# Two ties in the feed-forwards and another first block: a float32 decoder layer on one core

## The chip, the cores and the metric

The kernel runs on one core of one Trainium2 chip. Its engines are TensorE (PE in the profile; PEld is its weight load), VectorE (DVE), ScalarE (ACT), GpSimd (POOL) and SyncE (SP), the last two here mostly issuing transfers. The metric is the device time in microseconds of one execution, as the median of several. The time before is 1223.34 us (three runs, 1223.24 to 1223.8).

## The reference

One layer on 512 tokens of width 1024, all in float32:

```python
f = swiglu(rms_norm(h, ffn1_norm_pre[l]), ffn1_w_gate[l], ffn1_w_up[l], ffn1_w_down[l])
h = h + 0.5 * rms_norm(f, ffn1_norm_post[l])
u = rms_norm(h, mix_norm_pre[l])
proj = u @ w_in[l]
...                                  # dilated attention and a gated linear recurrence
h = h + rms_norm(merged @ w_out[l], mix_norm_post[l])
f = swiglu(rms_norm(h, ffn2_norm_pre[l]), ffn2_w_gate[l], ffn2_w_up[l], ffn2_w_down[l])
h = h + 0.5 * rms_norm(f, ffn2_norm_post[l])

def swiglu(x, w_gate, w_up, w_down):
    return (jax.nn.silu(x @ w_gate) * (x @ w_up)) @ w_down
```

The feed-forwards have 2816 hidden columns, 22 chunks of 128. The change lies in the two feed-forwards and in the very first block of the first.

## The kernel before

**Products.** A float32 matmul is made of three: each operand is split into a high part, which ScalarE writes with a rounding copy (`L269`), and a low part, which VectorE gets by subtraction (`L270`). TensorE adds high x high, high x low and low x high into one bank (`mm3`, L284 to L286; the same three at L1008 to L1010 and L922 to L924).

**The beginning.** The first six gate and up products go column block by column block of x, eight blocks k of 128. `fetch_start` loads for each k a weight block ("first" for k = 0, which also carries the gains, then "raw") and the rows `h`, all issued by SP in turn. Per k, ScalarE splits the weight, scales the rows by the gain into their high part (L361, `pre_norm`) and squares them for the norm; VectorE makes both low parts (L270, L362) and sums the squares. Four banks accumulate. Ahead of it, `WARM` matmuls on a constant tile (L1144, two rows of the trace each) keep TensorE busy while the first loads are under way.

**Chunks of a feed-forward.** From chunk f = 6 of the first (f = 3 of the second) gate and up of a chunk are computed together with seven half-size products instead of eight, in `prod`: p1, p5, p6, p2, p7, p3, p4, each twelve matmuls of 128x256. They share three banks. b takes p1, p6, p7, p4; z (bank 5) takes p5, then p3; y takes p2. Between them stand reads of a bank before the next product adds to it: ScalarE copies b to y after p1 (L1029), z to c5 after p5 and b to c6 after p6 (both L1016); VectorE reads b + c5 between p7 and p4 (L1021) and z + c6 after p3 (L1021). Thus p3 cannot begin before the copy c5 is taken, nor p4 before L1021 on b.

**Windows.** The down projection of the chunks already made is also done in seven products, in `step`, each on 128x512 rows (L922 to L924, banks 3, 4, 6, 7). Between two chunks there is a window of two or three of these steps. In the first feed-forward the first windows follow chunks 7 to 12 (the table `LEAD`: steps p1, p2, p5, then p6, p7, then p3, p4, and once more). Their weights come in by GpSimd's transfers into the tiles npair and dr, some of them adding to what lies there (L879, L881), and are split into `wd` (`down_form`) for the coming window, tied behind the copy c6.

**What sets the order.** A scheduler puts each engine's instructions in one fixed order, by priorities (`tc.high_priority`) and by when it reckons their inputs to be there. A tie, `tc.issue_after(i)`, forces what is issued inside it behind instruction i on i's engine. `behind(...)` ties to the last product (PE), the last silu (ACT) or the last gating multiply (DVE) of the chunk before:

```python
lead = f == n0
with behind("PE"):
    product("p1", b, True)
...
with behind("DVE", "ACT"):
    forms[ev[1]] = w_forms_in_place(("gu", n, ev[1]))
```

The first says that a chunk's p1 comes after the window ahead of it. The second holds back the weight forms of the next chunk: splits on ScalarE and VectorE (L269, L270) and sums on VectorE (L654 to L658). `last`, which the ties refer to, starts empty, so a feed-forward's first forms have no tie.

**The boundary.** Ahead of the second feed-forward, `Boundary.block` makes each of four token blocks: VectorE forms h (L475), ScalarE its sum of squares (L478), VectorE the normed rows u (L483). `Boundary.turn` transposes them on TensorE (L491), four matmuls to a bank and two banks to a block, and splits them (L494, L495, a copy L496). Blocks 2 and 3 are turned while the feed-forward's first products run on blocks 0 and 1 (`gemm_first`).

## Time and profile before

| | |
|---|---|
| median of three runs | 1223.34 us |
| the profiled execution's own time | 1223.28 us |
| its span | 1221.2 us |
| TensorE busy | 1209.9 us, 99% |
| VectorE busy | 984.0 us, 81% |
| ScalarE busy | 746.0 us, 61% |
| mean granted clock | 0.999 |

The span runs from the first instruction to the last; the own time holds 2.1 us more around it. A row of the timeline gives start, duration, engine, line, operation, output and input tiles with their shapes, and, in brackets, idle time of that engine just before with what ended it. Tile names carry no buffer numbers: `w`, `wd` and `bank` stand for several tiles each. Matmuls overlap, so a matmul's duration is longer than the distance to the next one's start.

### The profile page before, as it was taken

What the parts mean: (1) busy time and instruction counts of PE and PEld (TensorE: products, weight loads), DVE (VectorE), ACT (ScalarE), POOL (GpSimd) and SP (SyncE); (2) the same over time, 40 slices, a digit from 0 to 9 for tenths busy, and PEclk for the clock granted to TensorE, in tenths of its full rate; (3) what the DMA queues carried; (4) which work ended last, traced back from release to release, by engine and by line L of the source; (5) the groups of instructions that cost most, each with busy time, mean ns of one, the idle gap of its engine ahead of it and who ended that gap; (6) DMA issues with size and microseconds to landing.
All of it is one profiled execution on the core that took longest, in us unless ns stands there. A gap on an engine that the chain in (4) does not pass through costs nothing.

```text
span 1221.2 us, 19573 instructions
## 1 busy us (share of the span) xinstructions
PE 1209.9 (99%) x7790; PEld 1102.6 (90%) x7790; DVE 984.0 (81%) x1540; ACT 746.0 (61%) x1238; POOL 84.5 (7%) x139
## 2 busy tenths in 40 slices
PE   9999999999999999999999999999999999999998
PEld 8898989999878899999999888888899999999996
DVE  7998878988579888888776998755789887979864
ACT  6566665655656564666666788634566665656452
POOL 0001111100102000000001000000110110101000
PEclk9999999999999999999999999999999999999999
DMA  6336646464735222223235223524462655555441
GB/s 247 138 104 173 170 111 171 141 163 121 255 116 176 105 82 101 78 79 104 70 138 202 75 91 141 183 101 164 132 190 87 182 155 146 159 136 163 114 156 69
DMA packets 37452, 167.63 MB, mean 137 GB/s; under 512 B 4209, under 2 KB 7665, under 8 KB 25329
## 3 DMA queue, kind: packets, MB, share of 16 engines
q1 hardware_dynamic: 18432, 107.13, 25.2%
q0 software_dynamic: 18928, 59.25, 18.1%
q8 instruction: 61, 1.00, 0.3%
q14 instruction: 31, 0.25, 0.1%
HBM read 153.79 MB, written 8.39 MB: 133 GB/s over the span
## 4 chain that ended last, share of the span: by engine, by line
PE 93%; DVE 4%; issue 1%; DMA 1%; ACT 1%; DVEq 0%; ACTq 0%
PE bank L1008 10%; PE bank L1009 9%; PE bank L1010 9%; PE bank L284 7%; PE bank L286 7%; PE bank L285 7%; PE bank L675 6%; PE bank L676 6%; PE bank L677 6%; PE bank L923 4%; PE bank L922 4%; PE bank L924 4%; PE bank L405 3%; PE bank L406 3%; PE bank L404 3%; DVE w L270 1%
## 5 line engine op out<-in xcount | busy, mean ns | idle before, releaser
L270 DVE TENSOR_TENSOR w<-raw,w 128x1024 fp32r<-128x1024 f32 (+1 forms) x276 | 300.6, 1100 | 61.9 <-ACT w L269 56.0
L269 ACT ACTIVATE w<-raw 128x1024 fp32r<-128x1024 f32 (+1 forms) x276 | 258.9, 956 | 102.4 <-PE bank L286 40.1
L1008 PE MATMUL bank<-big,w 128*128 128x256 f32 x840 | 240.6, 286 | 2.5 <-ACT c L1016 0.9
L1009 PE MATMUL bank<-big,w 128*128 128x256 f32 x840 | 237.5, 283 | 0.0
L1010 PE MATMUL bank<-big,w 128*128 128x256 f32 x840 | 236.2, 283 | 0.0
L1008 PEld LDWEIGHTS bank<-big,w 128*128 128x128 f32 x840 | 160.8, 191 | 7.3 <-ACT c L1016 1.9
L1009 PEld LDWEIGHTS bank<-big,w 128*128 128x128 f32 x840 | 160.9, 192 | 1.6
L1010 PEld LDWEIGHTS bank<-big,w 128*128 128x128 f32 x840 | 160.3, 192 | 0.0
L922 PE MATMUL bank<-wd,act 128*128 128x512 f32 x224 | 87.8, 392 | 0.0
L923 PE MATMUL bank<-wd,act 128*128 128x512 f32 x224 | 87.8, 392 | 0.0
L924 PE MATMUL bank<-wd,act 128*128 128x512 f32 x224 | 87.2, 389 | 0.0
L675 PE MATMUL bank<-big,w 128*128 128x256 f32 x252 | 73.0, 290 | 0.0
L677 PE MATMUL bank<-big,w 128*128 128x256 f32 x252 | 71.5, 284 | 0.0
L676 PE MATMUL bank<-big,w 128*128 128x256 f32 x252 | 71.2, 283 | 0.0
L1016 ACT ACTIVATE c<-bank 128x256 f32<-128x256 f32 x72 | 27.5, 382 | 61.3 <-PE bank L1010 60.8
L270 DVE TENSOR_TENSOR wd<-npair,wd 128x1024 fp32r<-128x1024 f32 x24 | 29.4, 1224 | 37.7 <-ACT wd L269 37.7
L284 PE MATMUL bank<-act,w 128*128 128x512 f32 (+1 forms) x168 | 58.6, 354 | 0.0
L285 PE MATMUL bank<-act,w 128*128 128x512 f32 (+1 forms) x168 | 58.5, 349 | 0.0
L286 PE MATMUL bank<-act,w 128*128 128x512 f32 (+1 forms) x168 | 58.5, 349 | 0.0
L284 PE MATMUL bank<-big,w 128*128 128x512 f32 x144 | 56.0, 389 | 0.0
L285 PE MATMUL bank<-big,w 128*128 128x512 f32 x144 | 56.0, 389 | 0.0
L286 PE MATMUL bank<-big,w 128*128 128x512 f32 x144 | 56.0, 389 | 0.0
(399 smaller groups left out, 3208.7 us busy)
## 6 DMA issues: line engine op xcount, KB each, us to landing
raw<-in_w SPq DMA_DIRECT2D x90, 1024.0 KB, 4.9
dr<-in_wdn POOLq DMA_DIRECT2D x40, 512.0 KB, 5.8
npair<-in_wdn POOLq DMA_DIRECT2D x32, 512.0 KB, 5.5
big<-act POOLq DMA_DIRECT2D x6, 512.0 KB, 4.1
h<-in_x SPq DMA_DIRECT2D x8, 256.0 KB, 5.2
h<-in_xn POOLq DMA_DIRECT2D x4, 512.0 KB, 5.2
raw<-in_wbig SPq DMA_DIRECT2D x2, 1024.0 KB, 4.8
kept_m<-h POOLq DMA_DIRECT2D x4, 512.0 KB, 2.9
```

What stands on the lines that cost most here:

```text
L269: ACT.activation(dh, src, AF.Copy)
L270: DVE.tensor_sub(dl, src, dh.bitcast(F32))
L284: PE.matmul(ps, wh, xh, start=first, stop=False)
L285: PE.matmul(ps, wh, xl, start=False, stop=False)
L286: PE.matmul(ps, wl, xh, start=False, stop=last)
L675: PE.matmul(ps, wh, xh, start=start and k == 0, stop=False, skip_group_check=True)
L676: PE.matmul(ps, wh, xl, start=False, stop=False, skip_group_check=True)
L677: PE.matmul(ps, wl, xh, start=False, stop=k == 3, skip_group_check=True)
L922: PE.matmul(ps, xh, wh, start=start and k == 0, stop=False, skip_group_check=True)
L1008: PE.matmul(ps, wh, xh, start=start and k == 0, stop=False, skip_group_check=True)
L1009: PE.matmul(ps, wh, xl, start=False, stop=False, skip_group_check=True)
L1010: i = PE.matmul(ps, wl, xh, start=False, stop=k == 3, skip_group_check=True)
```

## The change

1. `WARM` falls from 10 to 8.
2. The load of the first rows (k = 0) is issued by ScalarE; all others stay on SP.
3. For k = 0 VectorE makes the rows' high part with a multiply (L1154 of the changed kernel), beside ScalarE's high part of the weight. ScalarE's squares stand behind its split, VectorE's low part of the rows behind the weight's.
4. For k = 0 and 1 TensorE takes the three kinds of product one after the other over all four banks (`by_kind`), no longer bank by bank.
5. In the first feed-forward, chunks that follow a window of three steps (f = 8 and f = 11) have their p1 free; their p3 is tied behind p7 in its place.
6. The second feed-forward's `last` starts with the last VectorE and ScalarE instruction of the last `turn`, so its first weight forms stand behind these.

```diff
-WARM = 10
+WARM = 8
...
-            nc.sync.dma_start(hm(k), xT[k])
+            (nc.sync if k else nc.scalar).dma_start(hm(k), xT[k])
...
-                DVE.tensor_sub(lo, src, hi.bitcast(F32))
-                ACT.activation(fb(b, FHALVES[i]), ps, AF.Copy)
+                i_dve = DVE.tensor_sub(lo, src, hi.bitcast(F32))
+                i_act = ACT.activation(fb(b, FHALVES[i]), ps, AF.Copy)
+            self.last = {"DVE": i_dve.ins, "ACT": i_act.ins}
...
-    def ffn(n, x, r, forms_x, home, pss):
+    def ffn(n, x, r, forms_x, home, pss, after={}):
...
-        last = {}
+        last = dict(after)
...
-            with behind("PE"):
+            early = n == 1 and len(LEAD.get(f - 1, ((), ()))[1]) > 2
+            with behind(*(() if early else ("PE",))):
                 product("p1", b, True)
...
-            product("p3", z, False)
+            with behind(*(("PE",) if early else ())):
+                product("p3", z, False)
...
+    def first_rows(x, wh, wl, raw):
+        g, xh, xl = col("g1a", 0), x.hi[0], x.lo[0]
+        DVE.tensor_scalar(xh, hm(0), g, None, op0=ALU.mult)
+        i = ACT.activation(wh, raw, AF.Copy)
+        with tc.issue_after(i.ins):
+            ACT.activation(acc, hm(0), AF.Square)
+        i = DVE.tensor_sub(wl, raw, wh.bitcast(F32))
+        with tc.issue_after(i.ins):
+            DVE.scalar_tensor_tensor(xl, hm(0), g, xh.bitcast(F32), op0=ALU.mult, op1=ALU.subtract)
+        by_kind(0, wh, wl, xh, xl)
+
+    def by_kind(k, wh, wl, xh, xl):
+        for w, v in ((wh, xh), (wl, xh), (wh, xl)):
+            for j in range(4):
+                PE.matmul(pss[j], w[:, j * P:(j + 1) * P], v, start=k == 0 and w is wh and v is xh, stop=False)
...
-    end2 = ffn(2, u2, None, forms_of(u2, his, los, ap2, True), home2, pss)
+    end2 = ffn(2, u2, None, forms_of(u2, his, los, ap2, True), home2, pss, bd2.last)
```

A tie moves instructions that its own lines don't name, so three places of the fixed order follow. Lines of the changed kernel are up to 3 higher around these places (L1016 is L1017 there, L1021 is L1022, L1029 is L1031).

ScalarE in the step f=8 of the first feed-forward; `c<-bank_78` is the copy c5 of z, `bank_75<-bank_73` the copy of b to y after p1, `c<-bank_73` the copy c6, `s` the window's copies out of banks 6 and 7. Before:

```order
L1016 ACTIVATE c<-bank_78 128x256
L934 ACTIVATE s_873<-bank_79 128x512
L269 ACTIVATE act<-ub 128x512
L934 ACTIVATE s_873<-bank_80 128x512
L1029 ACTIVATE bank_75<-bank_73 128x256
L1016 ACTIVATE c<-bank_73 128x256
```

and now:

```order
L1031 ACTIVATE bank_75<-bank_73 128x256
L935 ACTIVATE s_871<-bank_79 128x512
L935 ACTIVATE s_871<-bank_80 128x512
L1017 ACTIVATE c<-bank_78 128x256
L269 ACTIVATE act<-ub 128x512
L1017 ACTIVATE c<-bank_73 128x256
```

The copy after p1 moved to the front and c5 to behind the window's copies: on TensorE p1 now fills in between the window's last matmuls, then p5, and all twelve matmuls of p3 stand between p7 and p4, where three stood.

VectorE in the step f=11; `wd_98` and `wd_99` are the two down-weight splits, `ub<-bank_74,c` the read of b + c5 ahead of p4, `g<-bank_78,c` the read of z + c6. Before:

```order
L270 TENSOR_TENSOR act<-ub,act 128x512
L1021 TENSOR_TENSOR g<-bank_78,c 128x256
L270 TENSOR_TENSOR w_1415<-raw,w_1415 128x1024
L270 TENSOR_TENSOR wd_98<-npair,wd_98 128x1024
L1021 TENSOR_TENSOR ub<-bank_74,c 128x256
L270 TENSOR_TENSOR w_1414<-raw,w_1414 128x1024
L270 TENSOR_TENSOR wd_99<-dr_100,wd_99 128x1024
```

and now:

```order
L270 TENSOR_TENSOR act<-ub,act 128x512
L270 TENSOR_TENSOR wd_98<-npair,wd_98 128x1024
L270 TENSOR_TENSOR wd_99<-dr_100,wd_99 128x1024
L1022 TENSOR_TENSOR ub<-bank_74,c 128x256
L270 TENSOR_TENSOR w_1413<-raw,w_1413 128x1024
L1022 TENSOR_TENSOR g<-bank_78,c 128x256
L270 TENSOR_TENSOR w_1412<-raw,w_1412 128x1024
```

Both down-weight splits moved in front of the read that p4 waits for; one stood there before. On TensorE p1 and p5 fill the window here as in f=8, and eleven matmuls of f=12's p5, which stood between p7 and p4, moved behind p4.

ScalarE at the last turn ahead of the second feed-forward; `w<-raw` of 512 columns is the first weight form of its first chunk. Before:

```order
L383 ACTIVATE stat<-stat 128x1
L269 ACTIVATE w_8686<-raw 128x512
L478 ACTIVATE facc,stat<-h 128x1024
L494 ACTIVATE act<-bank_80 128x4x128
L390 ACTIVATE stat<-stat,eps 128x1
L494 ACTIVATE act<-bank_78 128x4x128
```

and now:

```order
L383 ACTIVATE stat<-stat 128x1
L478 ACTIVATE facc,stat<-h 128x1024
L494 ACTIVATE act<-bank_80 128x4x128
L390 ACTIVATE stat<-stat,eps 128x1
L494 ACTIVATE act<-bank_78 128x4x128
```

The form moved behind the last `L496`; on VectorE its low part and the two sums L654 and L655, which stood ahead of the block's L495, moved behind the last L495 likewise.

More of the change, by code (lines that the diff above doesn't have):

```diff
@@ L1147, in hybrid_layer @@
     r1 = npair[:, 1, :]
+    def first_rows(x, wh, wl, raw):
[12 more added lines that the diff above has]
+                PE.matmul(pss[j], w[:, j * P:(j + 1) * P], v, start=k == 0 and w is wh and v is xh, stop=False)
     for k in range(KC):
         wh, wl, raw = wts[k]
+        if k == 0:
+            first_rows(u1, wh, wl, raw)
+            continue
         split(wh, wl, raw)
         pre_norm(u1, "g1a", k, FULL)
-        sq_add(acc, lambda s: hm(k, s), FULL, k == 0)
+        sq_add(acc, lambda s: hm(k, s), FULL, False)
         if k == KC - 1:
             rstd(acc, r1, FULL)
+        if k == 1:
+            by_kind(k, wh, wl, u1.hi[k], u1.lo[k])
+            continue
         for j in range(4):
```

## The prediction

> **What bounds the kernel now.** I read the page's busy times first, then the waits of TensorE (line waited for, total us, times, longest):

> ```profile
> PE 1209.9 (99%) x7790; PEld 1102.6 (90%) x7790; DVE 984.0 (81%) x1540; ACT 746.0 (61%) x1238; POOL 84.5 (7%) x139
> PE bank L491 <- DVE u L483: 1.4, 1, 1.4
> PE bank L1008 <- ACT c L1016: 0.9, 2, 0.5
> PE bank L1008 <- DVE u L1021: 0.9, 1, 0.9
> ```

> TensorE is the bound, and its named waits are 3.2 us in four places. All four lie where the change moves something: L491 before the second feed-forward, L1008 in the first one's steps f=8 and f=11/12. So the question is how much of these holes closes, and what opens instead. A 128x512 matmul follows its neighbour after 0.23 us (18.08 to 18.31 below), a 128x256 one after 0.12 (112.68 to 112.80). Stretches of TensorE are counted with 0.2275 and 0.12; what a stretch is longer is a hole.

> **The beginning.** Timeline rows, two matmuls from later in the same stage, the first two loads with their us to landing, one row of stretches (core row: PE, PEld, DVE, ACT, POOL, clock, DMA share, GB/s) and the nearest row for the new VectorE instruction:

> ```profile
> 0.73 1.28 ACT L356 ACT_TABLE_LOAD   x1 [0.73 <-PEq L1735]
> 1.05 4.64 PE L1144 MATMUL bank<-ones 128*128 128x128 f32 x20 [1.05 <-DVE eps L201]
> 3.75 0.63 ACT L269 ACTIVATE w<-first 128x512 fp32r<-128x512 f32 x1 [1.43 <-DMA first<-in_first]
> 4.34 0.72 ACT L361 ACTIVATE act<-h,first 128x512 fp32r<-128x512 f32 x1
> 5.34 0.77 PE L284 MATMUL bank<-act,w 128*128 128x512 f32 x1
> ...
> 18.08 0.39 PE L284 MATMUL bank<-act,w 128*128 128x512 f32 x1
> 18.31 0.39 PE L285 MATMUL bank<-act,w 128*128 128x512 f32 x1
> first<-in_first SPq DMA_DIRECT2D x1, 292.0 KB, 3.0
> h<-in_x SPq DMA_DIRECT2D x1, 256.0 KB, 3.1
> 3.00:4.00 1.00, 1.00 (x7) 1.00 (x7) 0.00 (x0) 0.25 (x1) 0.00 (x0) 1.00 0.99 376
> L1383 DVE TENSOR_SCALAR facc<-facc,w 128x256 f32<-128x256 f32 x12 | 3.5, 349 | 0.0
> ```

> The weights ("first", issued 0.74) land at 3.74, the rows (issued 1.18) at 4.28. ScalarE splits one, then the other, and is done at 5.06; the first real matmul starts at 5.34, as the warm-up ends. Now ScalarE issues the rows at 0.73, in front of its table load; an issue row of SP lasts 0.38 to 0.43, so table load and warm-up activation end near 2.8 and hide in the 1.43 us that ScalarE waits for "first". The two high parts are then made side by side: weights on ScalarE (0.63), rows on VectorE (twice 0.349, 0.70 at most).

> Two bounds. If the second queue costs "first" nothing, the operands are there at 4.4 to 4.5 and the shorter warm-up (16 rows of 0.217, to 4.5) lets TensorE start at 4.6, 0.75 early. If both share the engines, both land at 4.28 and the start is about 5.1, 0.2 early. The DMA share of 0.99 in the fourth microsecond says that there is no idle engine to use: I take 0.2. A start that early runs at half pace (0.77 for a matmul that later takes 0.39), so it is worth half: **0.1 us**, 0.4 at the early bound. Below nothing: rows that land later than now, at the price of their delay, perhaps 0.2. The new order by kinds in the first two blocks moves no total, since TensorE finds its operands there already.

> [...]

> **Step f=8.** Rows of the timeline, and the landing of the transfer issued at 100.97:

> ```profile
> 97.84 0.39 PE L922 MATMUL bank<-wd,act 128*128 128x512 f32 x1
> 100.36 0.38 PE L1008 MATMUL bank<-big,w 128*128 128x256 f32 x1 [0.47 <-ACT c L1016]
> 100.97 0.87 POOL L879 DMA_DIRECT2D npair<-in_wdn  x1 [4.92 <-DVE wd L270]
> 107.43 1.05 ACT L269 ACTIVATE wd<-npair 128x1024 fp32r<-128x1024 f32 x1
> 110.79 0.42 DVE L1021 TENSOR_TENSOR u<-bank,c 128x256 f32<-128x256 f32 x1
> 111.27 0.39 PE L1008 MATMUL bank<-big,w 128*128 128x256 f32 x1 [0.92 <-DVE u L1021]
> 112.68 0.28 PE L1010 MATMUL bank<-big,w 128*128 128x256 f32 x1
> 112.80 0.40 PE L922 MATMUL bank<-wd,act 128*128 128x512 f32 x1
> npair<-in_wdn POOLq DMA_DIRECT2D x1, 512.0 KB, 5.4
> ```

> From 97.84 to 112.80 TensorE does 12 wide and 84 narrow matmuls, 2.73 + 10.08 = 12.81 of 14.96 us: 2.15 us of holes. Two are large. p3 follows p5 into bank 5 at once and waits for the copy c5 (at 100.36). Later only three matmuls of p3 are left between p7 and p4, and p4 waits for L1021, which stands on VectorE behind both down-weight splits (at 111.27).

> With the change p1 fills the window in place of p5, and all of p3 stands between p7 and p4. TensorE would reach p4 at 97.84 + 2.73 + 72 x 0.12 = 109.21. But L1021 still stands behind the two splits, and their first operand lands at 100.97 + 5.4 = 106.4; ScalarE now gets there earlier (p6 ends at 97.84 + 2.73 + 36 x 0.12 = 104.9, its copy c6 some 0.6 later) and waits for it. From ScalarE's split to p4 took 111.27 - 107.43 = 3.84; so p4 starts at 106.43 + 3.84 = 110.27. The hole before p4 stays 1.1 us, what ends it is now a DMA: gain 111.27 - 110.27 = **1.0 us**. Bounds: a landing after 5.6 gives 0.8; without that wait (c6 alone) 1.9.

> **Steps f=11 and f=12.** The same, with the transfers issued at 152.72, at the same place of a later window (1015.25), and at 145.50:

> ```profile
> 149.55 0.28 PE L1008 MATMUL bank<-big,w 128*128 128x256 f32 x1
> 152.72 0.86 POOL L879 DMA_DIRECT2D npair<-in_wdn  x1 [6.35 <-DVE wd L270]
> 160.22 1.05 ACT L269 ACTIVATE wd<-npair 128x1024 fp32r<-128x1024 f32 x1
> 164.64 0.40 PE L922 MATMUL bank<-wd,act 128*128 128x512 f32 x1
> 179.92 0.40 PE L922 MATMUL bank<-wd,act 128*128 128x512 f32 x1
> npair<-in_wdn POOLq DMA_DIRECT2D x1, 512.0 KB, 6.7
> npair<-in_wdn POOLq DMA_DIRECT2D x1, 512.0 KB, 5.5
> dr<-in_wdn POOLq DMA_DIRECT2D x1, 512.0 KB, 10.5
> ```

> 149.55 to 179.92 holds 36 wide and 168 narrow matmuls, 8.19 + 20.16 = 28.35 of 30.37: 2.0 us of holes, the largest again p3 behind c5. These close. But here L1021 moves: it stood behind one split, after eleven matmuls of f=12's p5; now it stands behind both, as in f=8. TensorE reaches p4 at 149.55 + 2.73 + 8.64 = 160.92. The transfer lands at 152.72 + 6.7 = 159.42, so p4 starts at 159.45 + 3.84 = 163.3: a new hole of 2.4, 2.5 with the 0.1 that a restart costs. Net 2.0 - 2.5 = **-0.5 us**. With the landing of 5.5 that this place shows in later windows it is p4 at 162.1 and +0.7. Nothing in the change touches the transfer or what precedes it, so I take its own row, 6.7. In f=12 the same L1021 keeps its one split and has all of p3 in front.

> **Before the second feed-forward.** Timeline rows:

> ```profile
> 880.86 1.28 DVE L475 SCALAR_TENSOR_TENSOR h<-facc,stat,h 128x1024 f32<-128x1024 f32 x1
> 883.52 0.63 ACT L269 ACTIVATE w<-raw 128x512 fp32r<-128x512 f32 x1 [4.18 <-DMA raw<-in_w]
> 884.05 1.04 ACT L478 ACTIVATE facc<-h 128x1024 f32<-128x1024 f32 x1
> 886.37 0.28 PE L284 MATMUL bank<-act,tx 128*128 128x256 f32 x1
> 887.77 1.41 DVE L483 SCALAR_TENSOR_TENSOR u<-h,stat,ub 128x512 f32<-128x512 f32 x2
> 888.66 0.63 PE L491 MATMUL bank<-cst,u 128*128 128x128 f32 x4 [1.42 <-DVE u L483]
> 889.33 0.63 PE L491 MATMUL bank<-cst,u 128*128 128x128 f32 x4
> 891.83 0.28 PE L284 MATMUL bank<-act,w 128*128 128x256 f32 x1
> ```

> ScalarE sits 4.18 us in front of a weight that is still under way, and the row sum L478, ready at 882.14, queues behind it. On VectorE the weight's three instructions then stand in front of the block's L495. The tie sends all that behind the last turn: L478 starts at 882.17, 1.88 earlier, and with the three out of VectorE's way L483 at about 885.6. The transposes followed it by 0.89 and 1.56: 886.5 and 887.2, the second done by 887.6, then the 24 matmuls of the tx product (2.88) to 890.46 instead of 891.83: **1.4 us**. Bounds 1.1 (VectorE keeps its spacing) and 1.8 (no wait at all). The moved instructions (0.63 on ScalarE, some 1.95 on VectorE) are first needed by f=3, over 20 us later; without that cover they would cost up to 1.95.

> **Sum** against the execution's own time: 0.1 + 1.0 - 0.5 + 1.4 = 2.0 us from 1223.28 (span 1221.2 and 2.1 around it), which is 0.06 under the median of the runs shown: **1221.3 us**. Off these places and its first microsecond the waits of TensorE list nothing, and what feeds it moves along with it.

> **Rivals.**

> *The late transfer is not late (35%).* f=11's transfer ends one engine's backlog from the load at 145.50 (10.5 us, until 156.0); where the next transfer starts later, 5.5 is shown. If the backlog is shorter, f=11 gives +0.7: 1223.3 - 3.2 = 1220.1, faster. Landings between give what lies between.

> *The pace steps up later (6%).* Two warm-up matmuls fewer end at 4.5, real ones start near 5.1: a gap of 0.6 us that is not there now. The row at 5.34 is still slow, so half pace lasts some 5 us from TensorE's first row (1.05). If the gap made that count start anew at 5.1, it would last to 10, some 4 us longer, worth 2.0: 1223.3, no change. Against it: the gap is an eighth of that time. [...]

> *The exposed transfer becomes the bound (6%, slower).* In f=11 each microsecond of landing now costs one: the sum is 2.0 at 6.7 us, nothing at 8.7. A landing like the 10.5 of the load before it gives a loss of 1.8: 1225.1. Until now ScalarE did another split first and came to wd only at 160.22, which hid it. Against it: the landings shown at this place are 5.4, 5.5 and 6.7.

> *The ties do not take (3%):* instructions stand as shown, but holes return elsewhere; 1223.

> The forecast has 50%. Within 0.2%, which is 2.45 us and about what a measurement of this kernel can tell from no change, lie three quarters of the forecast's share, a tenth of the first rival's, the second and the fourth: 0.48. Faster: a quarter of the forecast and nine tenths of the first rival, 0.45. Slower 0.07. The forecast's own spread is 1220.7 to 1222.0; eight in ten need the first rival's 1220.1 with the early start (0.3 less) and f=8's full gain for a part of it, and above it the lost warm-up: 1219.4 to 1223.0.

> **What would show it.** First real matmul near 5.1, "first" landing after 3.74. Steps f=8 and f=11: no wait for L1016; p4 waiting for L1021, and ScalarE's wd split with idle time ended by the DMA of npair. The transposes L491 at 886.5 less what came before, with a wait under 0.3. It is wrong if f=11's landing differs from 6.7, if L1021's place on VectorE does not bind, or if a hole opens at f=3 of the second feed-forward, where the moved splits are used.

## The result and the profile after

The change takes 1220.99 us, the median of 22 executions (1219.58 to 1223.56), beside 1223.27 us for the kernel before on the same chip (22 executions, 1222.74 to 1224.37). The ratio is 0.9983 with a 95% interval of 0.9978 to 0.9989: 2.3 us less. The interval excludes a ratio of 1, though the gain is a little under the 2.45 us that the forecast took for what a measurement can tell. The forecast was 1221.3 us. The time agrees; three of the four terms behind it do not.

The times of the change are not one heap: 13 executions lie from 1219.58 to 1221.58 and 9 from 1222.18 to 1223.56. The profiled execution is one of the latter, with an own time of 1222.24 us (span 1220.1), 1.04 less than the profiled execution before. So the two profiles show only that much of the gain, and why an execution falls in the upper group is part of the question.

From the page of the change, the busy times:

```profile
PE 1209.0 (99%) x7786; PEld 1102.6 (90%) x7786; DVE 983.7 (81%) x1541; ACT 745.0 (61%) x1237; POOL 84.3 (7%) x139
```

and what TensorE waits for (line waited for, total us, times, longest):

```profile
PE bank L1009 <- DVE ub L1022: 1.2, 1, 1.2
PE bank L1009 <- DVE u L1022: 1.1, 1, 1.1
PE bank L1147 <- DVE eps L201: 1.1, 1, 1.1
PE bank L1166 <- DVE act L1154: 0.9, 1, 0.9
```

The waits for the copy c5 and for the transposes' input are gone from the list. p4 now waits for VectorE's read in two places, where it waited in one before, and a new wait of 0.9 stands in front of the very first product. The start of the same matmul in both profiles says what each place gave:

| matmul | before | after | after minus before | given by the place |
|---|---|---|---|---|
| L349, in the first norm | 24.88 | 26.54 | +1.66 | 1.66 lost at the beginning |
| p4 of f=8 | 111.27 | 112.20 | +0.93 | 0.73 |
| first of a window after f=12 | 179.92 | 180.32 | +0.40 | 0.53 |
| first L491 ahead of the second feed-forward | 882.63 | 882.94 | +0.31 | 0.09 on the way |
| first L284 after the tx products | 891.83 | 890.76 | -1.07 | 1.38 |

Both ties gain, and the beginning loses. Timeline rows of the change for the beginning:

```profile
0.74 0.38 SPq L253 DMA_DIRECT2D first<-in_first  x1
0.74 0.40 ACTq L257 DMA_DIRECT2D h<-in_x  x1
1.06 3.78 PE L1147 MATMUL bank<-ones 128*128 128x128 f32 x16 [1.06 <-DVE eps L201]
4.95 0.63 ACT L1155 ACTIVATE w<-first 128x512 fp32r<-128x512 f32 x1 [2.19 <-DMA first<-in_first]
5.13 0.48 DVE L1154 TENSOR_SCALAR act<-h,first 128x512 fp32r<-128x512 f32 x1 [4.13 <-DMA h<-in_x]
```

its transfers issued at 0.74, with their us to landing,

```profile
first<-in_first SPq DMA_DIRECT2D x1, 292.0 KB, 4.2
h<-in_x ACTq DMA_DIRECT2D x1, 256.0 KB, 4.4
```

and stretches of 3.41 us of TensorE (us, busy and its rows, clock, DMA share, GB/s; the clock column reads 1.00 ahead of the first recorded change, so the pace is read from the rows):

```profile
2.42:5.83 3.41, 2.48 (x13) 1.00 0.93 318
5.83:9.24 3.41, 3.41 (x8) 1.00 1.04 378
9.24:12.65 3.41, 3.41 (x16) 1.00 1.05 399
```

The weights land 4.2 us after their issue; before it was 3.0. The warm-up ends at 1.06 + 16 x 0.217 = 4.53, and the first product starts at 5.77: TensorE is idle for 1.24 us. (The list of waits counts 0.9, from the end of the last warm-up row, which is later than the next row would have started.) Then it does 8 matmuls in 3.41 us where the next 3.41 us hold 16: full pace begins at 9.24 us. In the profile before it begins at 6.23, 3.0 us sooner; at half pace half of these 3.0 us is lost, 1.5 of the 1.66 in the table.

Timeline rows of the change for f=8 and f=11, the splits of the down weight, VectorE's read and p4:

```profile
102.62 0.87 POOL L880 DMA_DIRECT2D npair<-in_wdn  x1 [3.92 <-DVE wd L270]
108.36 1.06 ACT L269 ACTIVATE wd<-npair 128x1024 fp32r<-128x1024 f32 x1 [1.20 <-DMA npair<-in_wdn]
111.73 0.42 DVE L1022 TENSOR_TENSOR u<-bank,c 128x256 f32<-128x256 f32 x1
112.20 0.39 PE L1009 MATMUL bank<-big,w 128*128 128x256 f32 x1 [1.15 <-DVE u L1022]
153.64 0.86 POOL L880 DMA_DIRECT2D npair<-in_wdn  x1 [6.32 <-DVE wd L270]
159.38 1.06 ACT L269 ACTIVATE wd<-npair 128x1024 fp32r<-128x1024 f32 x1 [1.25 <-DMA npair<-in_wdn]
162.76 0.42 DVE L1022 TENSOR_TENSOR ub<-bank,c 128x256 f32<-128x256 f32 x1
163.23 0.39 PE L1009 MATMUL bank<-big,w 128*128 128x256 f32 x1 [1.20 <-DVE ub L1022]
```

ScalarE now waits for the transfer in both steps (1.20 and 1.25, ended by the DMA), and from its split to p4 it is 3.84 and 3.85 us, the 3.84 of the forecast. Both splits start 5.7 us after the issue of their transfer. Ahead of the second feed-forward:

```profile
882.48 1.06 ACT L478 ACTIVATE facc<-h 128x1024 f32<-128x1024 f32 x1 [2.84 <-DVE h L475]
885.86 1.41 DVE L483 SCALAR_TENSOR_TENSOR u<-h,stat,ub 128x512 f32<-128x512 f32 x2
886.75 1.29 PE L491 MATMUL bank<-cst,u 128*128 128x128 f32 x8
```

L478 now follows L475 and no weight stands in front of it; the eight transposes of both banks come in one piece and TensorE does not wait for them.

### The profile page after: what moved, and what is told of

Read it like the earlier page. It is cut to its first block, busy times and chain, and to the rows that moved or that the text cites. A ratio compares the mean times of both kernels' runs of the same rounds, so it can differ in the third digit from the quotient of the medians.

```text
span 1220.1 us, 19562 instructions
## 1 busy us (share of the span) xinstructions
PE 1209.0 (99%) x7786; PEld 1102.6 (90%) x7786; DVE 983.7 (81%) x1541; ACT 745.0 (61%) x1237; POOL 84.3 (7%) x139
## 4 chain that ended last, share of the span: by engine, by line
PE 96%; DVE 2%; DMA 1%; ACT 1%; issue 0%; DVEq 0%; ACTq 0%
PE bank L1009 9%; PE bank L1010 9%; PE bank L1011 9%; PE bank L284 7%; PE bank L285 7%; PE bank L286 7%; PE bank L676 6%; PE bank L677 6%; PE bank L678 6%; PE bank L923 4%; PE bank L924 4%; PE bank L925 4%; PE bank L405 3%; PE bank L404 3%; PE bank L406 3%; PE bank L750 1%
## 5 line engine op out<-in xcount | busy, mean ns | idle before, releaser
L270 DVE TENSOR_TENSOR w<-raw,w 128x1024 fp32r<-128x1024 f32 (+1 forms) x276 | 300.1, 1097 | 58.8 <-ACT w L269 52.7
L269 ACT ACTIVATE w<-raw 128x1024 fp32r<-128x1024 f32 (+1 forms) x276 | 258.3, 956 | 98.1 <-PE bank L286 45.4
L1010 PE MATMUL bank<-big,w 128*128 128x256 f32 x840 | 237.6, 283 | 0.0
L1010 PEld LDWEIGHTS bank<-big,w 128*128 128x128 f32 x840 | 160.9, 192 | 1.6
L1017 ACT ACTIVATE c<-bank 128x256 f32<-128x256 f32 x72 | 27.6, 383 | 56.0 <-PE bank L1011 55.4
L270 DVE TENSOR_TENSOR wd<-npair,wd 128x1024 fp32r<-128x1024 f32 x24 | 29.3, 1222 | 39.7 <-ACT wd L269 39.7
L284 PE MATMUL bank<-big,w 128*128 128x512 f32 x144 | 56.0, 389 | 0.0
L285 PE MATMUL bank<-big,w 128*128 128x512 f32 x144 | 56.0, 389 | 0.0
L284 PE MATMUL bank<-act,w 128*128 128x512 f32 (+1 forms) x160 | 55.5, 349 | 0.0
L285 PE MATMUL bank<-act,w 128*128 128x512 f32 (+1 forms) x160 | 55.4, 347 | 0.0
L286 PE MATMUL bank<-act,w 128*128 128x512 f32 (+1 forms) x160 | 55.4, 347 | 0.0
## 6 DMA issues: line engine op xcount, KB each, us to landing
dr<-in_wdn POOLq DMA_DIRECT2D x40, 512.0 KB, 5.6
npair<-in_wdn POOLq DMA_DIRECT2D x32, 512.0 KB, 5.5
big<-act POOLq DMA_DIRECT2D x6, 512.0 KB, 3.8
h<-in_xn POOLq DMA_DIRECT2D x4, 512.0 KB, 5.9
kept_m<-h POOLq DMA_DIRECT2D x4, 512.0 KB, 2.9
```

The source lines that it names most:

```text
L269: ACT.activation(dh, src, AF.Copy)
L270: DVE.tensor_sub(dl, src, dh.bitcast(F32))
L284: PE.matmul(ps, wh, xh, start=first, stop=False)
L285: PE.matmul(ps, wh, xl, start=False, stop=False)
L286: PE.matmul(ps, wl, xh, start=False, stop=last)
L1010: PE.matmul(ps, wh, xl, start=False, stop=False, skip_group_check=True)
```

## The experiments

Two questions: what makes the beginning fall in two groups, and whether p4 waits for the late transfer itself or only for its place in VectorE's order. Each time below stands beside executions of the kernel before on its own chip, whose medians were 1223.69 (first four kernels), 1223.57 (next four), 1223.47 (three) and 1224.22 us (the last).

### The ties alone, and the beginning alone

The first kernel is the one before with both ties (parts 5 and 6 of the change), the second the one before with parts 1 to 4.

```diff
 # ties alone, against the change
-WARM = 8
+WARM = 10
...
-            (nc.sync if k else nc.scalar).dma_start(hm(k), xT[k])
+            nc.sync.dma_start(hm(k), xT[k])
...
-        if k == 0:
-            first_rows(u1, wh, wl, raw)
-            continue
...
-        if k == 1:
-            by_kind(k, wh, wl, u1.hi[k], u1.lo[k])
-            continue
```

> The kernel before with the two ties alone (the step's read of the down product ahead of p1, and the second feed-forward behind the second half's last transposes); start, warm-up of 10 steps and the rows' load as before. If the ties gave what the two traces show after the start (0.7 at step 8, 0.5 to 0.7 at step 11, 1.36 before the second feed-forward, 2.6 to 2.7 in all), the times are one group at 1220.6, ratio 0.9978, and the new start is worth nothing even where the pace steps up in time. If the start has a gain of its own in its good executions, this kernel is above the lower group of the change, at 1220.8 or more; if the ties gave less, at 1221.5 or more.

> The kernel before with the new start alone (8 warm-up steps, the rows' load on ScalarE, the first rows' high part beside the weight's, the first two steps' products by kind); both ties left out. By theory GAP: two groups, near 1223.2 (step of the pace in time) and near 1225.0 (3 us late), ratio 1.0000 to 1.0015 by how many fall late; never under 1222.9. If the new start had the gain of 0.1 that was forecast and nothing else, one group at 1223.2.

Ties alone: 1220.84 us, 2.85 below before, ratio 0.9978 (0.9969 to 0.9987); a second timing gave 1220.73, 2.74 below, ratio 0.9982 (0.9972 to 0.9992). Beginning alone: 1225.21 us, 1.52 above before, ratio 1.0013 (1.0004 to 1.0022), eleven executions from 1223.81 to 1227.11. So the ties carry more than the whole gain, and the beginning takes some of it back; that it takes 0.5 in the change (2.3 against 2.8) and 1.5 alone is not settled. The expected two groups at 1223.2 and 1225.0 did not show as such.

The profile of the beginning alone held something else. Its stretches around the second feed-forward's start (TensorE busy, rows, clock, DMA share, GB/s):

```profile
885.58:888.99 3.41, 1.23 (x11) 1.00 0.59 157
888.99:892.40 3.41, 3.12 (x15) 0.50 0.82 255
```

and the rows of its timeline behind it:

```profile
884.14 0.63 ACT L269 ACTIVATE w<-raw 128x512 fp32r<-128x512 f32 x1 [5.26 <-DMA raw<-in_w]
884.67 1.04 ACT L478 ACTIVATE facc<-h 128x1024 f32<-128x1024 f32 x1
889.28 1.09 PE L491 MATMUL bank<-cst,u 128*128 128x128 f32 x4 [2.48 <-DVE u L483]
```

Without the second tie L478 still queues behind a weight under way. Here ScalarE waited 5.26 us for it where the profile before shows 4.18, the transposes waited 2.48 instead of 1.42, and after a stretch in which TensorE was busy for only 1.23 of 3.41 us the next 3.41 us were granted half the clock (0.50). This drop, at 888.99, lies 884.05 us behind the step to full pace at 4.93, 259 times 3.413 us (last section). In the kernel before, where full pace begins at 6.23, the stretch of that length, counted from there, that holds most of the hole, and the next:

```profile
886.87:890.29 3.42, 2.00 (x18) 1.00 0.55 146
890.29:893.70 3.41, 3.41 (x31) 1.00 0.95 305
```

There the stretch behind 2.00 us of work was granted 1.00. In this execution the beginning had been early (full pace at 4.93, matmuls at 882 0.45 us ahead of before), and its span is still 1.9 us longer: it lost 2.35 us from there on, 1.1 of them in the larger hole and the other 1.25 at half pace.

This stretch at half pace is hardly what puts the median 1.5 above before. A mean granted clock is on record for every execution, not only for profiled ones; a late first step doesn't show in it: the profile of the change, with full pace from 9.24 us, has 0.999 like that of before, with full pace from 6.23. This execution has 0.997, the ten others have 0.999. A late step at the beginning (1.66 in the profile of the change) would fit their times, but none of the ten was profiled.

### Each tie alone

```diff
 # step tie alone, against the ties alone
-    end2 = ffn(2, u2, None, forms_of(u2, his, los, ap2, True), home2, pss, bd2.last)
+    end2 = ffn(2, u2, None, forms_of(u2, his, los, ap2, True), home2, pss)
 # second tie alone, against the ties alone
-            early = n == 1 and len(LEAD.get(f - 1, ((), ()))[1]) > 2
+            early = False
```

> The tie of steps 8 and 11 alone, with the start of before and without the tie ahead of the second feed-forward. From the traces: 0.7 at step 8 and 0.5 to 0.7 at step 11, so 1.2 to 1.4 below before, ratio 0.9989; the forecast had 1.0 - 0.5 = 0.5 for it, ratio 0.9996. The hole ahead of the second feed-forward is 1.6 us as before, or more where the last weight block of the projection lands late.

> The tie ahead of the second feed-forward alone, with the start of before. The traces show 1.36 there: 1.4 below before, ratio 0.9989. Theory DIP (in the run with the new start alone a weight block landed 1.1 us later than in the profile of before, the hole grew from 1.6 to 2.6 us and TensorE ran at half pace for the next 3.41 us, so the tie also takes away a loss that only some executions have): the gain of the medians is over 1.4, up to 1.9, and the executions over 1.5 us above the middle are fewer than those of before. Without DIP the gain is 1.4 and the spread that of before.

Step tie alone: 1222.02 us, 1.55 below before, ratio 0.9992 (0.9983 to 1.0001), an interval that still contains 1. Second tie alone: 1221.87 us, 1.70 below, ratio 0.9985 (0.9977 to 0.9994). 1.70 is in the range of DIP, but the interval holds 1.4 too, and of 29 executions of before only one was over 1.5 us above its median, so how often the second tie also saves a stretch at half pace stays open.

The profiled execution of the step tie alone took 1225.19 us, 3.2 above its median, and shows what the exposed transfer can do. Its transfer at f=11, with the us to landing,

```profile
npair<-in_wdn POOLq DMA_DIRECT2D x1, 512.0 KB, 7.1
```

its timeline,

```profile
152.15 0.86 POOL L880 DMA_DIRECT2D npair<-in_wdn  x1 [6.28 <-DVE wd L270]
159.25 1.06 ACT L269 ACTIVATE wd<-npair 128x1024 fp32r<-128x1024 f32 x1 [2.59 <-DMA npair<-in_wdn]
163.09 0.39 PE L1009 MATMUL bank<-big,w 128*128 128x256 f32 x1 [2.54 <-DVE ub L1022]
```

and its stretches:

```profile
160.03:163.44 3.41, 0.87 (x8) 1.00 0.00 0
163.44:166.86 3.42, 3.42 (x16) 0.50 0.93 159
```

The landing took 7.1 us instead of 5.7, p4 waited 2.54, and the stretch behind that hole, in which TensorE was busy for 0.87 us, was granted 0.50: 1.4 + 1.7 = 3.1 of the 3.2 us. In the seven other profiles with this tie and the old order on VectorE the split began 5.4 to 5.7 us after the issue.

### The read ahead of the splits

At f=8, or at f=8 and f=11, the splits of the down weight are tied behind VectorE's read of p7's bank.

```diff
-                    DVE.tensor_add(dst, ps, c)
+                    last["sum"] = DVE.tensor_add(dst, ps, c).ins
...
+            if not early:
+                forms_due("copy")
             product("p7", b, False)
             sum_of(u[:, hi_], b, c5)
+            if early:
+                with tc.high_priority(offset=EVAC):
+                    forms_due("copy", "sum")
```

(`forms_due` is the loop over `down_form` that stood there; the kernel for f=8 alone adds `f == 8` to the condition.)

> The two ties with the start of before, and at steps 8 and 11 the splits of the down weight put behind the read of p7's bank on VectorE instead of ahead of it. In the changed kernel p4 waits 1.15 us at step 8 and 1.20 us at step 11 for that read, which stands behind splits whose transfer landed 5.7 us after its issue. Theory EXPOSED (the late transfer holds p4 only through the order on VectorE): both holes go, the splits now end about when the down products want them, gain 1.0 to 2.4 over the ties alone: 2.85 + 1.7 = 4.5 below before, ratio 0.9963. Rival BOUND (the transfer holds TensorE anyway, through the down products behind p4): the holes move behind p4, gain 0 to 0.5, ratio 0.9975.

> The two ties with the start of before, and the read of p7's bank ahead of the splits at step 8 alone, so that TensorE's order stays that of the ties alone. Theory EXPOSED: the hole ahead of p4 at step 8 (1.2 us) goes and nothing takes its place, that of step 11 (1.3 us) stays: 1.2 below the ties alone, 4.0 below before, ratio 0.9967. Rival BOUND: TensorE waits behind p4 for the down weight's splits instead, 0 to 0.4 below the ties alone.

> The kernel with the read first at both steps, timed again beside the ties alone (its first timing gave seven times). Its profile showed both holes ahead of p4 gone, 2.5 us, and new ones of 0.63 and 0.20 at step 12 and 0.60 at step 13, where TensorE's order has changed: 1.1 to 1.5 below the ties alone, ratio to before 0.9964 to 0.9968. If it is no better than the read first at step 8 alone, what step 11 gives is lost again at steps 12 and 13.

> The two ties alone again, as the base for the two kernels beside it on the same chip: 2.6 to 2.9 below before, ratio 0.9977.

Read first at both steps: 1219.21 us (six executions, and a seventh of 1979 us), 4.36 below before, ratio 0.9968 (0.9957 to 0.9979); again, beside the others, 1219.37 (five executions), ratio 0.9964 (0.9951 to 0.9976). At f=8 alone: 1219.38 us (five executions), ratio 0.9965 (0.9952 to 0.9979). The ties alone on the same chip: 1220.73. So the read first is worth 1.35, and f=11 adds nothing, as expected for the case that what it gives is lost at steps 12 and 13. The timeline of the kernel for f=8 alone:

```profile
100.36 0.87 POOL L880 DMA_DIRECT2D npair<-in_wdn  x1 [5.00 <-DVE wd L270]
105.81 1.06 ACT L269 ACTIVATE wd<-npair 128x1024 fp32r<-128x1024 f32 x1 [0.92 <-DMA npair<-in_wdn]
107.38 0.42 DVE L1022 TENSOR_TENSOR u<-bank,c 128x256 f32<-128x256 f32 x1 [1.23 <-PE bank L1011]
107.73 1.21 DVE L270 TENSOR_TENSOR wd<-npair,wd 128x1024 fp32r<-128x1024 f32 x1
159.46 0.38 PE L1009 MATMUL bank<-big,w 128*128 128x256 f32 x1 [1.11 <-DVE ub L1022]
```

The read follows p7 at once, the split starts after it, and TensorE has no wait at f=8 any more, neither at p4 nor in the window behind it; that of f=11 (1.11) stays. EXPOSED holds, BOUND falls: in this profile the transfer is not late for its own use, only for the instruction queued behind its split. In the kernel for both steps the hole at f=11 is gone as well, but the scheduler put thirteen matmuls of step 12 ahead of most of the down products, and new waits stand there:

```profile
178.19 0.38 PE L1009 MATMUL bank<-big,w 128*128 128x256 f32 x1 [0.47 <-ACT c L1017]
191.41 0.39 PE L1009 MATMUL bank<-big,w 128*128 128x256 f32 x1 [0.43 <-DVE ub L1022]
```

### The hole after the warm-up

Three kernels change only what TensorE does before the first product: the change with 11 warm-up steps (twice), the ties alone with 6, and the change with the first rows' load back on SyncE.

```diff
-WARM = 8
+WARM = 11
 # and, against the ties alone
-WARM = 10
+WARM = 6
 # and, against the change
-            (nc.sync if k else nc.scalar).dma_start(hm(k), xT[k])
+            nc.sync.dma_start(hm(k), xT[k])
```

> The changed kernel with 11 warm-up steps instead of 8 (22 rows of 128x512 instead of 16, at 0.217 us each), so that TensorE's warm-up ends near 5.83 us instead of 4.53 and covers the moment, 5.77, at which the first real product found its operands in the profile of the change; nothing else differs. Theory GAP (the 1.24 us hole between the warm-up and the first product puts the step of the pace off by 3.0 us in a part of the executions, which costs about half of it, 1.5 us, and makes the two groups of times, near 1220.6 and near 1222.5): the hole is gone, full pace begins near 6.2 us in every execution, the times make one group at 1220.6, ratio to before 0.9978. Theory PHASE (the step comes at a moment of its own, whatever the hole): the two groups stay, median between 1220.6 and 1222.5, and about 9 of 22 executions stand above 1222.

> The changed kernel with 11 warm-up steps again, since the first execution of it that was profiled ran at half pace from end to end and so shows no step. Theory GAP: no idle TensorE between 1.05 us and the first product, so the step of the pace stands between 4.1 and 6.5 us, as in the eight profiles with the 10 steps of before, and not near 9.1 to 9.9, as in three of four profiles with a hole; the median is 2.5 to 2.9 below before, ratio 0.9977 to 0.9980. Theory PHASE: the step can as well stand at 7 to 10 us and the median is 2.3 below before or less, ratio 0.9982 or more.

> The two ties with the start of before, but 6 warm-up steps instead of 10: 12 rows of 0.217 us from 1.05 end at 3.66, so that 1.7 us are idle before the first product at 5.34, whose operands come when they came before. Theory GAP (idle time in one of the 3.41 us windows of the pace keeps the step back by a window, which costs up to half of it): the step of the pace comes after 7.5 us in most executions, median 1.0 to 1.7 above the ties alone, ratio 0.9986 to 0.9992. Theory PHASE (the step comes where it comes): as the ties alone, ratio 0.9977, the step between 4.5 and 7.5 us.

> The changed kernel with the first rows' load issued by SyncE again, as before the change, 8 warm-up steps kept. The profile of before had the first weight block landing 3.0 us after its issue, that of the change 4.2 with the rows on ScalarE's queue beside it. Theory SHARING (the load on the second queue is what delays the block): the block lands after 3.0 us again, its high part starts near 3.8 instead of 4.95, the rows become the last operand, the hole after the warm-up (ends 4.53) falls to some 0.4 us or less, and by theory GAP the times are one group at 1220.4 (0.2 below the lower group of the change). If the landing is 4.2 whatever the queue, the hole stays over 1 us and the times stay in two groups, 1220.6 and 1222.5, or are worse by the rows' later issue.

The change with 11 steps: 1221.23 us (ten executions, and an eleventh of 2403 us), ratio 0.9983 (0.9974 to 0.9992), seven executions from 1220.25 to 1221.45 and three from 1223.09 to 1224.78. The three have a mean granted clock of 0.997, where no profile without a later stretch at half pace is under 0.998: they lost pace again after the beginning. The other seven are one group, as GAP has it, though above the expected 1220.6. (The trace shows the warm-up rows as 128x128, not as the 128x512 of the expectation.) The profiled execution is the one of 2403 us, 1.97 times the median of the ten; a 128x512 matmul in it follows its neighbour after 0.47 us (mean of 18, from 79.63 to 88.07) where it is 0.23 in the profile of before, and it shows no step. Timed again: 1220.91 us, all six from 1220.62 to 1221.30, 3.31 below a before of 1224.22, ratio 0.9971 (0.9959 to 0.9983). Its stretches:

```profile
0.20:3.61 3.41, 2.55 (x12) 1.00 0.45 132
3.61:7.02 3.41, 3.41 (x15) 1.00 1.05 379
7.02:10.43 3.41, 3.41 (x16) 1.00 1.04 373
```

No idle TensorE from 1.06 on, and full pace at 7.02. That is 2.2 us earlier than in the change but later than the 6.5 that was expected. The ties alone with 6 steps: 1221.91 us, 1.66 below before where 10 steps gave 2.85 and 2.74, so 1.1 to 1.2 are lost to a hole of 1.38 us (12 x 0.217 after 1.05 is 3.66, first product 5.04). Its stretches show the step one stretch late, as GAP has it:

```profile
3.09:6.50 3.41, 2.35 (x9) 1.00 1.02 347
6.50:9.91 3.41, 3.41 (x10) 1.00 1.00 369
9.91:13.32 3.41, 3.41 (x16) 1.00 1.06 410
```

The rows on SyncE: 1221.72 us, 1.97 below before, ratio 0.9981 (0.9972 to 0.9990), no better than the change. The landings were what SHARING expected:

```profile
first<-in_first SPq DMA_DIRECT2D x1, 292.0 KB, 2.8
h<-in_x SPq DMA_DIRECT2D x1, 256.0 KB, 3.0
```

but VectorE had the weight's low part ahead of the rows' high part in its order, the first product came at 5.50, and the hole was 0.97 instead of 0.4:

```profile
4.26 0.69 DVE L1158 TENSOR_TENSOR w<-first,w 128x512 fp32r<-128x512 f32 x1 [3.25 <-ACT w L1155]
4.87 0.48 DVE L1154 TENSOR_SCALAR act<-h,first 128x512 fp32r<-128x512 f32 x1
```

All profiles together:

| first product after a hole of | kernels | full pace from, us |
|---|---|---|
| 0 | before, and eight profiles with 10 or 11 steps | 4.06 to 7.02 |
| 0.74, of which 0.40 ahead of the step | beginning alone | 4.93 |
| 0.97 | rows on SyncE | 9.06 |
| 1.24 | the change | 9.24 |
| 1.38 | ties alone, 6 steps | 9.91 |

GAP fits these thirteen better than PHASE does: they spread over 5.85 us, but the nine starts without a hole over 2.96, less than one stretch of 3.41, and the three latest are those with holes of 0.97 us or more. That a hole puts the step off in some executions and not in others, by where it falls in a stretch, would be how one kernel comes to two groups of times; this is an estimate of the author's and was not shown. In the upper group of the change a late step is shown for the one profiled execution and not for the other eight. Their mean granted clock of 0.999 and 1.000 makes a later loss of pace, as in the three above, unlikely.

## Why the forecast was right, and where it was not

The likeliest case gave 1221.3 and 1220.99 was measured, but as 0.1 + 1.0 - 0.5 + 1.4 it was right by luck, by errors that cancel: too much at the beginning and at f=8, too little at f=11.

**The beginning (+0.1).** Wrong. The step that failed is the choice of the late bound: "both land at 4.28 and the start is about 5.1". Four profiles with the rows on ScalarE's queue show the weights landing after 3.7 to 4.2 us, ten with all on SyncE after 2.7 to 3.0, so both operands were there not at 4.28 but at 4.6 to 5.1, and the first product of the change started at 5.77. The rows' transfer was not hidden in the second queue, and the next weight block, which SyncE now issues at 1.18 in the place of the rows, runs beside both (4.5 us to its landing); with the rows back on SyncE the weights landed after 2.8 us. The rest is the rival "the pace steps up later", which had 6%: it happened in the profiled execution, with full pace 3.0 us later than before, 1.66 us by L349, and not the 4 us of a count that starts anew. The argument against it, that the gap is an eighth of the time, did not hold: the gap was 1.24 us and not 0.6, and half pace went on for one more stretch of 3.41 us behind one with 2.48 us of work. In the medians the beginning costs about 0.5 us, more than the 0.2 that the forecast put below nothing for rows that land late.

**f=8 (+1.0).** The mechanism holds to the hundredth: p4 comes 3.84 us after ScalarE's split, which waits for the transfer. The size was the landing, 5.7 us and not 5.4, so 0.73; the bound of 0.8 for a landing after 5.6 was the nearer one.

**f=11 and f=12 (-0.5).** Wrong in sign: +0.53 in the profile. The mis-sized term is the landing of 6.7 us, taken because it was that transfer's own row; it was 5.7 here and 5.4 to 5.7 in all other profiles of the tie but one. The first rival, the transfer that is not late (35%, +0.7 at a landing of 5.5), is what happened. One execution of another kernel with the tie shows 7.1 and p4 waiting 2.54 us, so the row of 6.7 was no mistake of reading but one draw: in the two other kernels without the tie of f=8 and f=11, the beginning alone and the second tie alone, the same transfer landed after 5.4 and 5.7. With it the rival of the exposed transfer (6%) exists as an event: 3.2 us in that execution, of which 1.7 were not foreseen, the stretch granted 0.50 behind the hole. Five of the 22 executions of the ties alone (1223.12 to 1224.88) have a mean granted clock of 0.996 or 0.997 and so lost pace somewhere; that it was here was not profiled.

**The second feed-forward (+1.4).** Right: 1.38 by the traces. L478 was forecast at 882.17, L483 at 885.6 and the transposes at 886.5; at the +0.31 of this place they come at 882.48, 885.86 and 886.75. Timed alone the tie gave 1.70, and no hole opened where the moved splits are used.

**The sum.** In the medians the ties give 2.7 to 2.9 where 1.9 was forecast, and the beginning takes 0.5 where 0.1 was added. The upper end of the range, 1223.0 for the lost warm-up, lies 1.7 us above the likeliest case; no trace of before shows such a term, and the profile of the change showed 1.66. The break-even landing of 8.7 us for the transfer counted only the wait; with a stretch at half pace behind it, as at the landing of 7.1 (1.7 us), it lies lower. The chances written as 0.48, 0.45 and 0.07 come to 0.50, 0.44 and 0.06 by the forecast's own list.

## What to carry to other kernels

A transfer that landed late (5.7 us) held up here what was queued behind its first reader, VectorE's read and with it p4 (a wait of 1.15 us at f=8), and not only its user: when an earlier start uncovers such a transfer, put the short reads that free a bank ahead of the split that waits for it (1.35 us here, for a transfer that was in time for its own use). Size a warm-up so that it ends after the latest landing seen of the first operands, not after the earliest hoped for: three warm-up steps more cost nothing that could be measured, and in three profiles holes of 0.97 to 1.38 us came with full pace only from beyond 9 us (1.1 to 1.2 us in the medians for the one of 1.38). Look also at the granted clock behind a hole in TensorE's work: here the stretches behind one with 1.23 and one with 0.87 of 3.41 us busy were granted 0.50, which cost 1.25 and 1.7 us more, and that behind one with 2.00 was granted 1.00.

The fastest kernels found have the old beginning, both ties and the read first, at f=8 alone (1219.38 us, 4.1 below before and 1.35 below the ties alone) or at both steps (1219.37): the two can't be told apart.

## What the runs showed of the hardware

```profile
1208.97:1212.38 3.41, 1.72 (x15) 1.00 0.40 154
1210.52:1213.93 3.41, 1.50 (x13) 1.00 0.40 154
```

The first is of the kernel with the read first at f=8, and its next stretch was granted 1.00; the second is of the second timing of the ties alone, and its next was granted 0.50. At the beginning, half pace went on behind stretches with 2.35, 2.48, 2.55 and 2.76 us busy, and full pace began behind this one with 3.00:

```profile
0.65:4.06 3.41, 3.00 (x14) 1.00 0.66 198
4.06:7.47 3.41, 3.36 (x19) 1.00 1.02 342
```

(stretches of the kernel with the read first at f=8.) So the full clock was still granted behind a stretch with 1.72 us of work, and not yet behind one with 2.76 at the beginning; whether the work in a stretch is what decides it was not tried.

One execution took 2403 us, with a 128x512 matmul every 0.47 us where the profile of before has one every 0.23, and one of another kernel took 1979 us at a mean granted clock of 0.556; why was not found.
